# The order of the first DMA loads on SyncE and ScalarE: two quarters of unit 0 ahead of the positions and frequencies

## Chip, cores, metric

The kernel runs on one core of a Trainium2 chip. The metric is the time on the device in microseconds (us), as a median of several runs. A profile shows one execution, from its first to its last instruction. This span is 1.7 to 2.1 us shorter than the time of the same execution, and times inside a profile count from its start.

## The reference, cut to what matters

```python
# x (8, 8, 1024, 64) float32, freqs (32,), positions 0..1023, scale 0.5
angles = np.outer(positions * scale, freqs)
cos, sin = np.cos(angles), np.sin(angles)
x_first, x_second = x[..., :32], x[..., 32:]
out_first  = x_first * cos - x_second * sin
out_second = x_first * sin + x_second * cos
```

16.8 MB are read and 16.8 MB are written. The table of sines and cosines comes out of two tiny inputs, 8 KB of positions and 128 bytes of frequencies, and everything else waits for it.

## The kernel before

x is cut into four units of 128 rows by 8192 elements. GpSimd's DMAs convert to float16 while they load. Only the second half of unit 0 is loaded as float32, in two quarters of 1 MB by SyncE and ScalarE, into X0f; ScalarE converts it later. `pin` fixes the order of the instructions on their engine.

```python
    X0f = xout.tile([P, N], FP32, tag="O")
    Q = NH // 2                                    # 2048 elements, 8 KB of each row
    pin(nc.sync.dma_start(out=X0f[:, :Q], in_=xv[0][:, NH : NH + Q]))        # SyncE's quarter

    pos_i64 = consts.tile([P, K8], positions.dtype)
    pin(nc.scalar.dma_start(out=pos_i64, in_=positions.rearrange("(p k) -> p k", k=K8)))
    freq_row = consts.tile([1, half], FP32)
    pin(nc.scalar.dma_start(out=freq_row, in_=freqs[None, :]))
    pin(nc.scalar.dma_start(out=X0f[:, Q:NH], in_=xv[0][:, NH + Q :]))       # ScalarE's quarter
    ...
    pin(nc.gpsimd.dma_start(out=Xf[0][:, :NH], in_=xv[0][:, :NH]))           # first half of unit 0
    ...  # constants by GpSimd
    for u in range(1, NU):                         # units 1 to 3, the last one in two pieces
        ...
        pin(nc.gpsimd.dma_start(out=Xf[u][:, : N - c], in_=xv[u][:, : N - c]))
    ...
    # cfreq = coef x freq_row (TensorE); posf = float(positions); y = posf * cfreq (VectorE)
    # tab = sines and cosines (ScalarE); T = tab spread over the rows (TensorE, copies by ScalarE, VectorE)
    pin(nc.scalar.copy(out=Xf[0][:, NH:], in_=X0f[:, :NH]))
    for u in range(NU):
        for s in range(2):                         # half units
            ...                                    # four VectorE operations, then OUT <- X on ScalarE
            # stores: units 0 and 3 by SyncE for each half, units 1 and 2 by GpSimd as a whole
```

The positions are 128 records of 64 bytes, one for each row, eight on each of the 16 DMA engines. A quarter is 128 records of 8 KB, also eight for each engine.

Of the kernel before, what the change touches and what calls it, by code (L numbers as in the profile page):

```python
# [21 lines left out]
def kernel(  # L22
# [8 lines left out]
    nc = tc.nc  # L31
    pin = tc.keep_in_program_order
# [11 lines left out]
    NH = KH * D  # L44
    K8 = S // P
# [7 lines left out]
    xv = x.rearrange("b h s d -> (b h s d)").rearrange("(u p n) -> u p n", p=P, n=N)  # L53
# [11 lines left out]
    X0f = xout.tile([P, N], FP32, tag="O")  # L65
    Q = NH // 2
    pin(nc.sync.dma_start(out=X0f[:, :Q], in_=xv[0][:, NH : NH + Q]))

    pos_i64 = consts.tile([P, K8], positions.dtype)
    pin(nc.scalar.dma_start(out=pos_i64, in_=positions.rearrange("(p k) -> p k", k=K8)))  # L70
    freq_row = consts.tile([1, half], FP32)
    pin(nc.scalar.dma_start(out=freq_row, in_=freqs[None, :]))
    pin(nc.scalar.dma_start(out=X0f[:, Q:NH], in_=xv[0][:, NH + Q :]))

    X = [xin.tile([P, K, 2, half], FP16, name=f"X{u}") for u in range(NU)]
    Xf = [t.rearrange("p k h j -> p (k h j)") for t in X]
# [12 lines left out]
        out=one, in_=one, compare_op=ALU.not_equal, fill=1.0, base=0,  # L89
        pattern=[[-1, G], [-G, HP]], channel_multiplier=1,  # L90
    ))
    for u in range(1, NU):
# [12 lines left out]
        out=posf, in_=pos_i64.bitcast(I32).rearrange("p (k t) -> p k t", t=2)[:, :, 0]  # L105
# [3 lines left out]
        out=y,  # L109
# [8 lines left out]
        out=r, in0=m, scalar=_MAGIC, in1=y, op0=ALU.subtract, op1=ALU.subtract  # L118
# [5 lines left out]
        out=ra.bitcast(I32), in0=r.bitcast(I32), scalar1=0x7FFFFFFF, scalar2=None, op0=ALU.bitwise_and  # L124
# [5 lines left out]
    for g in range(0, G, 2):  # L130
        ps = spread.tile([P, 2, 2, W], FP32, tag="g")
        for i in range(2):
            nc.tensor.matmul(  # L133
                out=ps[:, i].rearrange("p t w -> p (t w)"),
# [12 lines left out]
    for u in range(NU):  # L147
        OUT = xout.tile([P, N], FP32, tag="O")
        for s in range(2):
# [9 lines left out]
                out=Xs[:, :, 0, :], in0=Xs[:, :, 0, :], in1=pr[:, :, 1, :], op=ALU.subtract  # L159
            ))  # L160
            pin(nc.vector.tensor_tensor(  # L161
                out=Xs[:, :, 1, :], in0=pr[:, :, 0, :], in1=Xs[:, :, 1, :], op=ALU.add
# [39 lines left out]
```

## Time and profile before

| | before |
|---|---|
| time, median of 6 runs | 84.39 us (84.19 to 84.59) |
| span of the profile | 82.4 us |
| busy: VectorE, ScalarE, TensorE | 60.3, 40.1, 6.0 us |
| shares of the three DMA queues together | 97.3% of the span |

VectorE works back to back in the middle of the span, and the DMA engines are full almost from end to end. The lines that carry this stand in the prediction. The queues: q0 is GpSimd's, q1 SyncE's, q10 ScalarE's (the prediction calls the last two the HWDGE rings); a ring is what one queue has on one DMA engine. The columns are packets, MB written, and share of the 16 engines' time.

```profile
q1 hardware_dynamic: 720, 9.44, 27.5%
q10 hardware_dynamic: 290, 1.06, 3.3%
```

### The profile page before, as it was taken

The page shows a single profiled execution, that of the slowest core. Times are in us where ns is not written, and L with a number is a line of the kernel's source. Part 1 is how long each engine was busy: PE and PEld are TensorE (multiplying, and loading weights), DVE is VectorE, ACT ScalarE, POOL GpSimd, SP SyncE. Part 2 cuts the span into 40 slices and gives each one's busy share as a digit, 9 for nine tenths or more (in the row PEclk, how much of TensorE's full clock was granted, in tenths as well). Part 3 has the DMA queues.
Part 4 walks back from the last instruction along what each step waited for, and adds up shares of the span by engine and source line. Part 5 has one row for each costly group of instructions (what it writes and reads, how often), then busy time and mean ns, then how long its engine had stood idle before and what let it go on. Part 6 is the DMA issues. An engine that isn't in the chain of part 4 may idle for free.

```text
span 82.4 us, 183 instructions
## 1 busy us (share of the span) xinstructions
PE 6.0 (7%) x18; PEld 2.4 (3%) x18; DVE 60.3 (73%) x40; ACT 40.1 (49%) x18; POOL 5.1 (6%) x15
## 2 busy tenths in 40 slices
PE   0011797100000000000000000000000000000000
PEld 0011232000000000000000000000000000000000
DVE  0306277999999999999999999999999998000000
ACT  0602259999950690294088049309705911950000
POOL 4950000000000000000000200000110000000000
PEclk9999999995555555555555555555555555555555
DMA  2899997996996999899899899997995998989992
GB/s 44 345 312 286 282 350 167 255 255 143 239 255 127 255 255 334 302 308 280 239 322 266 239 398 330 545 430 334 509 509 255 509 509 350 414 382 469 422 414 95
DMA packets 2018, 26.22 MB, mean 318 GB/s; under 512 B 354, under 2 KB 354, under 8 KB 482
## 3 DMA queue, kind: packets, MB, share of 16 engines
q0 software_dynamic: 1008, 15.73, 66.5%
q1 hardware_dynamic: 720, 9.44, 27.5%
q10 hardware_dynamic: 290, 1.06, 3.3%
HBM read 16.79 MB, written 16.78 MB: 407 GB/s over the span
## 4 chain that ended last, share of the span: by engine, by line
DVE 54%; ACT 15%; issue 7%; DMA 6%; PE 5%; DVEq 1%; ACTq 0%
DVE X L157 20%; DVE pr L156 20%; DVE X L161 9%; DMA freq_row<-in_freqs_dram 6%; ACT T L143 5%; DVE X L158 5%; ACT OUT L164 4%; ACT X L144 4%; PE ps L133 4%; DVEq L197 1%; PE cfreq L101 1%; ACT tab L126 1%; DVE r L117 1%; DVE y L108 1%; ACTq L70 0%
## 5 line engine op out<-in xcount | busy, mean ns | idle before, releaser
L164 ACT CAST OUT<-X 128x4096 f32<-128x4096 f16 x8 | 28.8, 3606 | 24.2 <-DVE X L161 24.2
L156 DVE TENSOR_TENSOR pr<-X,T 128x4096 f16<-128x4096 f16 x8 | 18.3, 2292 | 0.8 <-ACT T L143 0.5
L157 DVE TENSOR_TENSOR X<-X,T 128x4096 f16<-128x4096 f16 x8 | 18.3, 2292 | 0.3
L158 DVE TENSOR_TENSOR X<-X,pr 128x2048 f16<-128x2048 f16 x8 | 9.8, 1224 | 0.3
L161 DVE TENSOR_TENSOR X<-pr,X 128x2048 f16<-128x2048 f16 x8 | 9.7, 1217 | 0.0
L143 ACT CAST T<-ps 128x1024 f16<-128x1024 f32 x6 | 5.7, 1030 | 2.4 <-PE ps L133 2.4
L133 PE MATMUL ps<-tab,sel 128*128 128x512 f16 x16 | 5.4, 489 | 2.8 <-ACT tab L126 2.2
L168 POOL DMA_DIRECT2D out_dram<-OUT x2 | 1.1, 537 | 53.7 <-ACT OUT L164 53.7
L141 DVE CAST T<-ps 128x1024 f16<-128x1024 f32 x2 | 2.4, 1224 | 2.2 <-PE ps L133 2.2
L144 ACT CAST X<-X0f 128x4096 f16<-128x4096 f32 x1 | 3.6, 3650 | 0.0
L99 DVE COPY sel<-one 128x2048 f16<-128x2048 f16 x1 | 0.7, 693 | 2.8 <-POOL one L88 2.8
L121 ACT ACTIVATE tab<-r 128x256 f16<-128x256 f32 x1 | 0.4, 416 | 4.4 <-DVE r L117 4.4
L121 ACT ACT_TABLE_LOAD x1 | 1.3, 1283 | 2.1 <-issue 2.1
L133 PEld LDWEIGHTS <-sel 128*128 128x128 f16 x16 | 1.9, 120 | 5.9 <-issue 5.3
L94 POOL DMA_DIRECT2D X<-in_x_dram x3 | 2.0, 659 | 0.0
L104 DVE CAST posf<-pos_i 128x8 f32<-128x8 int32 x1 | 0.2, 171 | 2.1 <-DMA pos_i<-in_positions_dram 2.1
L101 PE MATMUL cfreq<-freq_row,coef 1*128 1x32 f32 x2 | 0.6, 392 | 5.9 <-DMA freq_row<-in_freqs_dram 5.9
L108 DVE TENSOR_TENSOR y<-posf,cfreq 128x256 f32<-128x256 f32 x1 | 0.4, 423 | 0.7 <-PE cfreq L101 0.7
L84 POOL DMA_DIRECT2D X<-in_x_dram x1 | 0.7, 667 | 0.8 <-POOLq L183 0.8
L101 PEld LDWEIGHTS cfreq<-freq_row,coef 1*128 1x128 f32 x2 | 0.5, 306 | 5.9 <-issue 5.9
L96 POOL DMA_DIRECT2D X<-in_x_dram x1 | 0.6, 558 | 0.0
L126 ACT ACTIVATE tab<-ra,quarter 128x256 f16<-128x256 f32 x1 | 0.5, 507 | 0.0
(11 smaller groups left out, 2.3 us busy)
## 6 DMA issues: line engine op xcount, KB each, us to landing
out_dram<-OUT SPq DMA_DIRECT2D x4, 2048.0 KB, 14.2
out_dram<-OUT POOLq DMA_DIRECT2D x2, 4096.0 KB, 14.8
X<-in_x_dram POOLq DMA_DIRECT2D x2, 2048.0 KB, 25.7
X<-in_x_dram POOLq DMA_DIRECT2D x1, 1792.0 KB, 44.6
X0f<-in_x_dram SPq DMA_DIRECT2D x1, 1024.0 KB, 4.7
X<-in_x_dram POOLq DMA_DIRECT2D x1, 1024.0 KB, 11.5
X0f<-in_x_dram ACTq DMA_DIRECT2D x1, 1024.0 KB, 13.4
X<-in_x_dram POOLq DMA_DIRECT2D x1, 256.0 KB, 47.7
```

Of the source, the lines that this page charges most:

```text
L94: pin(nc.gpsimd.dma_start(out=Xf[u][:, : N - c], in_=xv[u][:, : N - c]))
L101: nc.tensor.matmul(out=cfreq, lhsT=coef, rhs=freq_row, start=True, stop=True)
L121: pin(nc.scalar.activation(out=tab[:, 0], in_=r, func=AF.Sin, bias=0.0, scale=-_TWO_PI_DN))
L133: nc.tensor.matmul(out=ps[:, i].rearrange("p t w -> p (t w)"), lhsT=sel[:, g + i].rearrange("s h q -> s (h q)"), rhs=tab.rearrange("s t k ...
L141: pin(nc.vector.tensor_copy(out=dst, in_=ps))
L143: pin(nc.scalar.copy(out=dst, in_=ps))
L144: pin(nc.scalar.copy(out=Xf[0][:, NH:], in_=X0f[:, :NH]))
L156: pin(nc.vector.tensor_tensor(out=pr, in0=Xs, in1=sin_b, op=ALU.mult))
L157: pin(nc.vector.tensor_tensor(out=Xs, in0=Xs, in1=cos_b, op=ALU.mult))
L158: pin(nc.vector.tensor_tensor(out=Xs[:, :, 0, :], in0=Xs[:, :, 0, :], in1=pr[:, :, 1, :], op=ALU.subtract))
L161: pin(nc.vector.tensor_tensor(out=Xs[:, :, 1, :], in0=pr[:, :, 0, :], in1=Xs[:, :, 1, :], op=ALU.add))
L164: pin(nc.scalar.copy(out=OUT[:, ns], in_=Xf[u][:, ns]))
```

## The change

The intent: both issuing engines begin at once with a large transfer, and ScalarE's quarter no longer stands behind two small loads.

```diff
     pin(nc.sync.dma_start(out=X0f[:, :Q], in_=xv[0][:, NH : NH + Q]))
+    pin(nc.scalar.dma_start(out=X0f[:, Q:NH], in_=xv[0][:, NH + Q :]))
 
     pos_i64 = consts.tile([P, K8], positions.dtype)
-    pin(nc.scalar.dma_start(out=pos_i64, in_=positions.rearrange("(p k) -> p k", k=K8)))
+    pin(nc.sync.dma_start(out=pos_i64, in_=positions.rearrange("(p k) -> p k", k=K8)))
     freq_row = consts.tile([1, half], FP32)
     pin(nc.scalar.dma_start(out=freq_row, in_=freqs[None, :]))
-    pin(nc.scalar.dma_start(out=X0f[:, Q:NH], in_=xv[0][:, NH + Q :]))
```

## The prediction

> **What bounds the kernel now.** I read the chain of waits first, because the change touches only the first six microseconds and the question is whether those lie on it.
>
> ```profile
> 1.16 4.61 DMA freq_row<-in_freqs_dram
> 5.90 0.61 PE cfreq L101 x2
> 6.54 0.43 DVE y L108
> ...
> 8.74 3.38 PE ps L133 x8
> 12.14 3.08 ACT T L143 x4
> ...
> 16.82 3.50 ACT X L144
> 20.35 2.31 DVE pr L156
> ...
> 69.67 3.60 ACT OUT L164
> ```
>
> Columns: start, length (us), work. The end is tied rigidly to the landing of the 128-byte frequencies: cfreq, y, the sine table, its spreading by TensorE, the copies into T, the conversion of X0f (L144), and from 20.35 on VectorE back to back. So what delays y delays everything behind it. The timeline names the other input of y, and what the first rotation waits for:
>
> ```profile
> 5.63 0.17 DVE L104 CAST posf<-pos_i 128x8 f32<-128x8 int32 x1 [2.14 <-DMA pos_i<-in_positions_dram]
> 6.54 0.42 DVE L108 TENSOR_TENSOR y<-posf,cfreq 128x256 f32<-128x256 f32 x1 [0.74 <-PE cfreq L101]
> 13.19 2.29 DVE L156 TENSOR_TENSOR pr<-X,T 128x4096 f16<-128x4096 f16 x1 [0.47 <-ACT T L143]
> 16.67 3.65 ACT L144 CAST X<-X0f 128x4096 f16<-128x4096 f32 x1
> ```
>
> Positions came 0.3 us before the frequencies; either can become the gate. L144 has no wait on its line: ScalarE is busy with T until then, and X0f is there already. Next the transfers, by issue and by stretch (last two columns of the second view: DMA share, GB/s written):
>
> ```profile
> X<-in_x_dram POOLq DMA_DIRECT2D x1, 1024.0 KB, 11.5
> X0f<-in_x_dram SPq DMA_DIRECT2D x1, 1024.0 KB, 4.7
> X0f<-in_x_dram ACTq DMA_DIRECT2D x1, 1024.0 KB, 13.4
> pos_i<-in_positions_dram ACTq DMA_DIRECT2D x1, 8.0 KB, 4.9
> ```
>
> ```profile
> 1.75:5.80 4.05, 0.00 (x0) 0.00 (x0) 0.86 (x2) 1.28 (x1) 3.37 (x9) 1.00 1.02 332
> 5.80:13.20 7.40, 4.83 (x14) 2.12 (x15) 3.90 (x7) 2.97 (x5) 0.00 (x0) 1.00 1.03 278
> 20.40:69.65 49.25, 0.00 (x0) 0.00 (x0) 48.56 (x28) 25.07 (x7) 1.07 (x2) 0.50 1.01 335
> 73.30:82.40 9.10, 0.00 (x0) 0.00 (x0) 0.00 (x0) 0.00 (x0) 0.00 (x0) 0.50 0.81 346
> ```
>
> The 16 DMA engines are full from 1.75 us nearly to the end, so the kernel stands close to two limits: compute and its last store, and a DMA backlog. The two quarters, equal in size, take 4.7 and 13.4 us: a transfer costs what its place in its ring and its neighbours cost, not what its bytes cost.
>
> **What the Trainium skill says.** "DMA: Bandwidth & Descriptors", section "Queues, rings and completion order": each of the 16 engines has one ring per queue, consumes a ring in order, and goes round-robin over the rings that have work, one packet per turn. The trace's packet records agree. Until about 4.7 us each engine alternates an 8 KB packet of SyncE's quarter with a 64-byte packet of the positions, one for one, although one takes 0.31 us and the other 0.01. Later it alternates ScalarE's quarter with GpSimd's load. Near 13.3 us an 8 KB packet is followed by one 1.21 us GpSimd packet before the 4-byte completion of the same ring gets its turn. So **a turn costs what the neighbour's packet costs, however small one's own is.** The same page, section "Why a DMA increments its semaphore by 16 and not by 1": only the full count means that all has landed. Hence the slowest engine counts for the positions (128 rows, eight on each engine); the frequencies are one record on one engine. Same page, "Latency and other measured facts": first byte about 1 us for GpSimd's DMA. The trace doesn't agree here: issued at 1.25, its first packet starts at 4.71.
>
> **The change, part by part.**
>
> Removed: positions (0.39 us of issuing) and frequencies (0.55) no longer stand ahead of ScalarE's quarter, which is issued at 0.74 instead of 1.74. Nothing on the chain waits for that quarter, so its gain is zero.
>
> Added: positions behind SyncE's quarter, frequencies behind ScalarE's. No compute instruction changes; VectorE, TensorE and GpSimd have the same order as before, and ScalarE and SyncE differ only in those issues.
>
> Cost, as seen by one middling engine, with packet times from the records (8 KB plain 0.31 us; 8 KB written by the casting load, which reads twice that, 0.61; 16 KB written by it 1.21):
> - First packets from about 2.0. Before, eight plain packets were through by 4.8; now these eight are four of each quarter. I assume that GpSimd's load enters at 4.75, as before.
> - Four rounds of all three rings, 0.61 + 0.31 + 0.31 = 1.23 us each: both quarters end at 9.7.
> - The quarters' completion packets need a turn behind the fifth GpSimd packet: 10.3.
> - Positions one to three follow GpSimd's packets six to eight, at 10.9, 11.5, 12.1. The fourth comes with that load's own completion. Then GpSimd's ring goes on with unit 1, whose packets take 1.21: positions five to eight at 13.3, 14.5, 15.8, 17.0, and their completion at 18.2. Slowest engine and landing add about 0.5, so 18.7.
> - If GpSimd enters one round later, one 1.21 turn drops out: about 17.5. I take **18.3 for the positions, against 5.6**.
> - Frequencies need only two turns behind their quarter on one engine: about 12.
>
> Then posf (0.17) and gaps: y starts at about 18.5 instead of 6.54, **a shift of 12.0 us**. Everything on the chain behind it keeps its lengths. GpSimd's loads go on during this, so X never becomes the wait.
>
> At the end: the last store is issued at 73.3 + 12.0 = 85.3. Alone it would need about 1.0 to start, 8 x 0.62 = 5.0 per engine, and 0.4 to land: 91.7, where before it landed at 81.5. But backlog remains: unit 2's store is issued at 59.5 + 12.0 = 71.5, starts perhaps 2 us later (estimate, between the skill's 1 and the 3.5 seen), and from there 16 + 8 + 8 packets of 0.62 = 19.8 us end at 93.3, landing at 93.7. With the 0.9 us that follow the last landing in the trace before, the span is 94.6. The timed runs lie 1.95 above the span (84.35 against 82.4): 96.5. Without that backlog: 94.6. I put **96.2**.
>
> **Rivals.**
> - *The small transfers slip in early.* If GpSimd's load can't enter while the HWDGE rings have work, both quarters run at the 0.31 us pace and end near 7.3, with positions and frequencies at about 7.5. For it: on each engine GpSimd's first packet directly follows the end of SyncE's quarter, as if it had waited for that; and it started late. Against it: from 5.4 to 12.4 it alternates one for one with ScalarE's quarter, which never ran empty in that time. Also, a newcomer waits behind packets already scheduled: the first store, issued at 23.86, has its first packet only at 28.5, behind two or three loads. The shift would be 1 to 1.5 us; the last store now ends some 1.8 us later than it would alone, so most of that would hide: 84.3 to 85.7, within 2%.
> - *Earlier X0f gains time.* ScalarE's quarter lands at some 10 instead of 15.2 us. But L144 starts when ScalarE is free at 16.67, and its order on ScalarE is fixed behind the copies into T. Gain nil; this is the only way to faster and I see nothing for it.
> - *The delay is hidden by DMA.* The engines were the second limit, and work moved from the start isn't lost. But stores depend on compute: all loads together are about 39 us of engine time, done by about 42, while the second store comes at 43 and the third only at 57, so the engines run dry for several us before unit 1's store. This can hide no more than the 1.8 us above.
>
> **Range and chances.** Given turn-taking with three rings (I hold it for 85% likely), entry of GpSimd's load a round earlier or later moves the shift to 11 to 13, and the backlog moves the end by 2: 93.5 to 98.5. The first rival is most of the rest. Range 92.5 to 98.8; slower by over 2% 0.86, within 2% 0.12, faster 0.02.
>
> **What would show it.** The wait of posf on the positions grows from 2.14 to about 15 us, and the chain begins with positions in place of frequencies. Issue to landing: positions some 17 us, SyncE's quarter near 9 instead of 4.7, ScalarE's about 9 instead of 13.4. Between 5 and 18 us PE, VectorE and ScalarE show almost nothing; behind it the same groups with the same mean durations, and slices with low DMA share in the second half. What would make it wrong: positions landing by 8 us (the first rival), or frequencies later than positions.

## The result

The changed kernel takes 95.13 us (94.7 to 95.24, 6 runs) against 84.39 for the one before. The ratio is 1.126, with a 95% interval of 1.123 to 1.129. Here and below a ratio is the mean time of one kernel's runs over that of the other's of the same rounds, so it is not quite the ratio of the medians. Executions over 1.5% slower than the fastest of the same kernel are left out of the means.

The chain of waits of the changed kernel (start, length, work) begins with the positions:

```profile
1.18 16.77 DMA pos_i<-in_positions_dram
...
17.97 0.18 DVE posf L104
...
18.25 0.43 DVE y L108
...
20.44 3.59 PE ps L133 x8
...
32.26 2.30 DVE pr L156
```

Before, y began at 6.54; now it begins at 18.25, 11.71 us later. From there on the links are the same. The timeline of the changed kernel shows that the frequencies were not the gate, and how far the first rotation has moved:

```profile
10.89 0.60 PE L101 MATMUL cfreq<-freq_row,coef 1*128 1x32 f32 x2 [10.89 <-DMA freq_row<-in_freqs_dram]
17.97 0.17 DVE L104 CAST posf<-pos_i 128x8 f32<-128x8 int32 x1 [14.48 <-DMA pos_i<-in_positions_dram]
...
25.09 2.29 DVE L156 TENSOR_TENSOR pr<-X,T 128x4096 f16<-128x4096 f16 x1 [0.67 <-ACT T L143]
```

The frequencies were there 7 us before the positions, whose wait on VectorE grew from 2.14 to 14.48 us. The first rotation starts 11.90 us later than before (25.09 against 13.19). The 0.2 us more than at y fell to TensorE's spreading of the table, whose matmuls took 596 ns in the mean instead of 489.

The transfers of the changed kernel, with the time from issue to landing in the last column:

```profile
X0f<-in_x_dram ACTq DMA_DIRECT2D x1, 1024.0 KB, 10.0
X0f<-in_x_dram SPq DMA_DIRECT2D x1, 1024.0 KB, 9.9
...
pos_i<-in_positions_dram SPq DMA_DIRECT2D x1, 8.0 KB, 16.8
```

The two quarters, 4.7 and 13.4 us before, now take the same time, as two rings in turn would. ScalarE's quarter is on the chip 4.4 us earlier (0.74 + 10.0 against 1.74 + 13.4), and nothing uses it: its conversion starts at 28.57. The queues of the changed kernel:

```profile
q1 hardware_dynamic: 864, 9.45, 24.6%
q10 hardware_dynamic: 146, 1.05, 2.8%
```

Exactly 144 packets have moved from q10 to q1, with 0.01 MB: 128 records of positions and 16 completions. Each record is a packet of its own. The packet records of the trace show the turns. As medians over the 16 engines, SyncE's quarter ends at 9.0 and ScalarE's at 9.3; a position follows at 10.5, 11.1, 11.7, each behind a 0.62 us packet of GpSimd's first load, two at 12.2 and 12.4, where that load ends, and then one at 13.5, 14.8 and 16.0, each behind a packet of unit 1 of some 1.2 us. Their completion, a 4-byte packet that reports the landing, goes at 17.2; on the slowest engine it goes at 17.6.

The end grew less than the start: the span by 11.0 us, the first rotation by 11.9. The kernel before had a backlog of transfers at its end that hid 0.9. Behind it the DMA engines now run dry, as this stretch of the changed kernel and then of the one before shows (the last two columns are the DMA share and GB/s written; each share is the mean over the 18 us, in which nearly idle stretches and full ones alternate):

```profile
57.00:75.00 18.00, 0.00 (x0) 0.00 (x0) 17.73 (x12) 7.63 (x4) 1.07 (x2) 0.50 0.71 304
```

```profile
57.00:75.00 18.00, 0.00 (x0) 0.00 (x0) 12.47 (x8) 9.40 (x3) 0.53 (x1) 0.50 0.97 419
```

### The profile page after: what moved, and what is told of

Read it like the earlier page. It is cut to its first block, busy times and chain, and to the rows that moved or that the text cites. A ratio compares the mean times of both kernels' runs of the same rounds, so it can differ in the third digit from the quotient of the medians.

```text
span 93.4 us, 183 instructions
## 1 busy us (share of the span) xinstructions
PE 7.1 (8%) x18; PEld 2.8 (3%) x18; DVE 60.3 (65%) x40; ACT 40.1 (43%) x18; POOL 5.1 (6%) x15
## 4 chain that ended last, share of the span: by engine, by line
DVE 48%; DMA 18%; ACT 13%; issue 6%; PE 4%; DVEq 1%; SPq 0%; ACTq 0%
DMA pos_i<-in_positions_dram 18%; DVE X L157 17%; DVE pr L156 17%; DVE X L161 8%; ACT T L143 4%; DVE X L158 4%; ACT OUT L164 4%; PE ps L133 4%; ACT X L144 4%; DVEq L197 1%; ACT tab L126 1%; DVE r L117 0%; DVE y L108 0%; SPq L67 0%; ACT tab L121 0%
## 5 line engine op out<-in xcount | busy, mean ns | idle before, releaser
L156 DVE TENSOR_TENSOR pr<-X,T 128x4096 f16<-128x4096 f16 x8 | 18.3, 2292 | 1.0 <-ACT T L143 0.7
L157 DVE TENSOR_TENSOR X<-X,T 128x4096 f16<-128x4096 f16 x8 | 18.3, 2292 | 0.3
L133 PE MATMUL ps<-tab,sel 128*128 128x512 f16 x16 | 6.5, 596 | 8.9 <-ACT tab L126 8.9
L101 PE MATMUL cfreq<-freq_row,coef 1*128 1x32 f32 x2 | 0.6, 390 | 10.9 <-DMA freq_row<-in_freqs_dram 10.9
L101 PEld LDWEIGHTS cfreq<-freq_row,coef 1*128 1x128 f32 x2 | 0.5, 308 | 10.9 <-issue 10.9
## 6 DMA issues: line engine op xcount, KB each, us to landing
out_dram<-OUT POOLq DMA_DIRECT2D x2, 4096.0 KB, 11.7
```

The costliest lines, as they stand in the source:

```text
L133: nc.tensor.matmul(out=ps[:, i].rearrange("p t w -> p (t w)"), lhsT=sel[:, g + i].rearrange("s h q -> s (h q)"), rhs=tab.rearrange("s t k ...
L156: pin(nc.vector.tensor_tensor(out=pr, in0=Xs, in1=sin_b, op=ALU.mult))
L157: pin(nc.vector.tensor_tensor(out=Xs, in0=Xs, in1=cos_b, op=ALU.mult))
```

## The experiments

Theory: the positions pay one neighbour's packet for each of their own packets, however small they are; they were through early before because SyncE's plain 8 KB packets (0.31 us) were the only neighbour, and they pay GpSimd's packets (0.61, then 1.21 us) now. Rivals: the wait is one for bytes, or for a share of the bandwidth; or the mere place behind a quarter is what costs, for the frequencies as well. All eight kernels compute the right result, and each was timed over three rounds.

### The neighbour's packets made smaller

```diff
     for u in range(1, NU):
         c = C2 if u == NU - 1 else 0
+        if u == 1:
+            for b in range(0, N, N // 4):
+                pin(nc.gpsimd.dma_start(out=Xf[u][:, b : b + N // 4], in_=xv[u][:, b : b + N // 4]))
+            continue
```

> The changed kernel, with GpSimd's load of unit 1 in four pieces by columns: the same bytes, ring and order, but packets of 4 KB written (0.31 us) in place of 16 KB (1.21 us). Theory (the positions pay a neighbour's packet for each turn; four of their turns fell behind unit 1's packets): positions land 4 x 0.9 = 3.6 us earlier, near 14.3 instead of 17.95, time about 91.5 us (90.5 to 92.5). Rival (the positions wait for bytes ahead of them or for their share of the bandwidth, which are unchanged): 95 us.

Measured: 91.44 us, ratio 1.084 to the kernel before. The positions landed 12.9 us after their issue instead of 16.8:

```profile
14.13 0.17 DVE L108 CAST posf<-pos_i 128x8 f32<-128x8 int32 x1 [10.64 <-DMA pos_i<-in_positions_dram]
```

That is 3.84 us earlier than in the changed kernel, where the theory said 3.6, and the time fell by 3.7. The same bytes in the same order on the same ring: the bandwidth rival has no place for this.

### The positions cut into twice as many packets

```diff
-    pin(nc.sync.dma_start(out=pos_i64, in_=positions.rearrange("(p k) -> p k", k=K8)))
+    pv = positions.rearrange("(p k) -> p k", k=K8)
+    pin(nc.sync.dma_start(out=pos_i64[:, : K8 // 2], in_=pv[:, : K8 // 2]))
+    pin(nc.sync.dma_start(out=pos_i64[:, K8 // 2 :], in_=pv[:, K8 // 2 :]))
```

> The changed kernel, with the positions (still 8 KB in all) loaded by two DMAs of four columns each, both behind SyncE's quarter: 16 small packets and two completions on each engine instead of 8 and one. Theory (turns): nine more turns behind GpSimd's 1.21 us packets, 10.9 us: positions land near 28.9 instead of 17.95, time 105 to 107 us. Rival (the wait is set by the quarter ahead and by bytes): within 1 us of 95.

Measured: 105.55 us, ratio 1.249.

```profile
27.61 0.17 DVE L106 CAST posf<-pos_i 128x8 f32<-128x8 int32 x1 [24.12 <-DMA pos_i<-in_positions_dram]
```

The same 8 KB came 9.64 us later and the time grew by 10.4; of the other 0.7, 0.4 lie behind the last conversion (8.7 us from there to the end instead of 8.3), where nothing was changed and what made it longer was not looked for, and 0.3 outside the span. So it is the number of packets that counts, not the bytes. The nine turns expected would have been 10.9 us; the landing shows eight (9.64 / 1.21 = 8.0). The packet records show where the ninth is: near 21.9 one turn fell on the 4-byte completion of unit 1's load instead of a 1.21 us packet, which I had overlooked.

### The neighbour held back

GpSimd reads one column of posf before it issues its loads, so it can't enter before the positions are in.

```diff
-    pin(nc.gpsimd.dma_start(out=Xf[0][:, :NH], in_=xv[0][:, :NH]))     # and the loop over units 1 to 3
 ...
+    gate = consts.tile([P, 1], FP32)
+    pin(nc.gpsimd.tensor_copy(out=gate, in_=posf[:, :1]))
+    pin(nc.gpsimd.dma_start(out=Xf[0][:, :NH], in_=xv[0][:, :NH]))     # then the loop
```

> The changed kernel, with all of GpSimd's loads held back until posf is made (GpSimd reads one column of it first). Theory (the positions wait for GpSimd's packets, not for the quarters): both quarters end near 7.0, positions land at about 7.5 instead of 17.95, y at about 7.8. The price is an idle stretch of the DMA engines of some 2 us from 7.1 to 9.2, since GpSimd's first packet comes about 1.1 us after its issue: time 85.3 to 87.5 us. Rival (a small transfer of 64-byte records is slow behind any quarter): positions well beyond 10 us, time above 90.

Measured: 87.79 us, ratio 1.041. The wait of the positions and the stretch of the DMA engines after it:

```profile
8.40 0.17 DVE L98 CAST posf<-pos_i 128x8 f32<-128x8 int32 x1 [6.09 <-DMA pos_i<-in_positions_dram]
```

```profile
7.30:10.10 2.80, 0.60 (x2) 0.60 (x3) 1.41 (x5) 0.07 (x1) 1.47 (x4) 1.00 0.04 3
```

Behind the same quarter, without GpSimd's packets, the positions land at 8.4 instead of 17.95. That settles who makes them wait. The time missed its forecast by 0.3 us: I had put the idle stretch at 2 us, and it was 2.8 with a slow start behind it (first packets of 0.76 to 1.62 us in place of 0.62). The loss against the kernel before is 3.4 us. It is no longer the positions' doing: the first rotation now waits for GpSimd's own load, held back, and starts 3.5 us later than before (16.67 against 13.19):

```profile
16.67 2.29 DVE L159 TENSOR_TENSOR pr<-X,T 128x4096 f16<-128x4096 f16 x1 [1.70 <-DMA X<-in_x_dram]
```

### Only one of the two small loads moved

With the positions ahead again:

```diff
+    pin(nc.sync.dma_start(out=pos_i64, in_=...))        # ahead of SyncE's quarter
     pin(nc.sync.dma_start(out=X0f[:, :Q], ...))
     pin(nc.scalar.dma_start(out=X0f[:, Q:NH], ...))
-    pin(nc.sync.dma_start(out=pos_i64, in_=...))
     pin(nc.scalar.dma_start(out=freq_row, in_=freqs[None, :]))
```

> The changed kernel, but the positions stand ahead of SyncE's quarter again; the frequencies stay behind ScalarE's quarter. Theory (the positions were the gate of the changed kernel; the frequencies need two turns only): positions land by about 6 us, the frequencies near 10.8 as in the changed kernel, and they become the gate: y at about 11.5 instead of 18.25 (before: 6.54), time 88.4 us (87.5 to 89.5). Rival (both small transfers cost about the same; the harm is that something small is behind a quarter at all): close to 95 us.

With the frequencies ahead again:

```diff
+    pin(nc.scalar.dma_start(out=freq_row, in_=freqs[None, :]))   # ahead of ScalarE's quarter
     pin(nc.sync.dma_start(out=X0f[:, :Q], ...))
     pin(nc.scalar.dma_start(out=X0f[:, Q:NH], ...))
     pin(nc.sync.dma_start(out=pos_i64, in_=...))
-    pin(nc.scalar.dma_start(out=freq_row, in_=freqs[None, :]))
```

> The changed kernel, but the frequencies stand ahead of ScalarE's quarter again; the positions stay behind SyncE's quarter. Theory: the frequencies had 7 us to spare in the changed kernel, so nothing changes: positions land near 17.5 to 18, y at about 18, time 94 to 95.5 us. Rival (the frequencies cost something of their own): visibly below 95, by 2 us or more.

Both expectations failed. Measured: 84.25 us with the positions ahead (ratio 0.999) and 84.24 with the frequencies ahead (0.999), the time of the kernel before. The transfers of the first of them (positions ahead), then of the second:

```profile
X0f<-in_x_dram ACTq DMA_DIRECT2D x1, 1024.0 KB, 4.7
X0f<-in_x_dram SPq DMA_DIRECT2D x1, 1024.0 KB, 11.6
...
pos_i<-in_positions_dram SPq DMA_DIRECT2D x1, 8.0 KB, 2.8
```

```profile
X0f<-in_x_dram SPq DMA_DIRECT2D x1, 1024.0 KB, 4.6
...
X0f<-in_x_dram ACTq DMA_DIRECT2D x1, 1024.0 KB, 11.4
...
pos_i<-in_positions_dram SPq DMA_DIRECT2D x1, 8.0 KB, 4.3
```

In each, one quarter took 4.6 or 4.7 us, as if it were alone. In the second the positions stand behind SyncE's quarter just as in the changed kernel, and landed 4.3 us after their issue instead of 16.8. The issues of the quarters suggest why (start and length; first with the positions ahead, then with the frequencies ahead):

```profile
0.74 0.40 ACTq L70 DMA_DIRECT2D X0f<-in_x_dram  x1
...
1.16 0.43 SPq L69 DMA_DIRECT2D X0f<-in_x_dram  x1
```

```profile
0.74 0.37 SPq L69 DMA_DIRECT2D X0f<-in_x_dram  x1
...
1.30 0.36 ACTq L70 DMA_DIRECT2D X0f<-in_x_dram  x1
```

The later ring's first 8 KB packet came at 4.71 and 4.83, when the earlier ring's quarter was through. So the quarter that led by 0.42 or 0.56 us had the engines to itself, and what stood behind it went out before GpSimd's load came in at 5.2. With the frequencies ahead, the positions did not even pay a turn each: all 128 records went between 4.76 and 5.05, and in that time ScalarE's quarter, issued at 1.30, began at most one 0.31 us packet on each engine. So the turn for each record is what the changed kernel and its first two variants show, and no rule for every busy neighbour. My expectations had simply carried over the turn-taking of the changed kernel, where both quarters are issued at 0.74.

### The same two with the quarters issued together again

If that is so, one more small load that nobody reads, ahead of the other quarter, must bring the loss back.

```diff
     # to the kernel with the frequencies ahead
+    freq_idle = consts.tile([1, half], FP32)
+    pin(nc.sync.dma_start(out=freq_idle, in_=freqs[None, :]))           # ahead of SyncE's quarter
     # to the kernel with the positions ahead
+    pos_idle = consts.tile([P, K8], positions.dtype)
+    pin(nc.scalar.dma_start(out=pos_idle, in_=positions.rearrange("(p k) -> p k", k=K8)))   # ahead of ScalarE's
```

> As e2_freq_first (frequencies ahead of ScalarE's quarter, positions behind SyncE's), with one more 128-byte load, into a tile that nobody reads, ahead of SyncE's quarter, so that both quarters are issued in the same moment again (near 1.3 us). New theory (a ring that starts half a microsecond earlier gets the engines to itself until its quarter is through at about 4.8; only quarters issued together take turns, end after GpSimd's load has entered, and leave the positions to its packets): positions land near 17.5 to 18.5, time 94 to 96 us. Rival (positions behind a quarter are harmless as long as the frequencies are ahead of the other one): 84.2 us, as e2_freq_first.

Measured: 94.70 us, ratio 1.122. A 128-byte load that nobody reads costs 10.5 us:

```profile
17.25 0.17 DVE L106 CAST posf<-pos_i 128x8 f32<-128x8 int32 x1 [13.76 <-DMA pos_i<-in_positions_dram]
```

> As e1_pos_first (positions ahead of SyncE's quarter, frequencies behind ScalarE's), with a second load of the positions, into a tile that nobody reads, ahead of ScalarE's quarter, so that both rings carry the same again and both quarters are issued near 1.2 us. New theory: the quarters take turns, the frequencies come two turns behind the end of ScalarE's at 11 to 12.5 us and are the gate: y at 11.6 to 13, time 88.5 to 90.5 us. Rival (frequencies behind a quarter are harmless as long as the positions are ahead of the other one): 84.3 us, as e1_pos_first.

Measured: 89.93 us, ratio 1.068:

```profile
12.00 0.60 PE L103 MATMUL cfreq<-freq_row,coef 1*128 1x32 f32 x2 [12.00 <-DMA freq_row<-in_freqs_dram]
```

Both hold in time, and the frequencies also in y (12.64, said 11.6 to 13); the positions of the first landed at 17.23, 0.3 us before their range. The quarters of the first were level only in part, for SyncE's was still issued 0.14 us ahead:

```profile
1.14 0.36 SPq L71 DMA_DIRECT2D X0f<-in_x_dram  x1
...
1.28 0.37 ACTq L72 DMA_DIRECT2D X0f<-in_x_dram  x1
```

In the second kernel the frequencies alone are behind, and their price with turn-taking quarters is seen by itself: y at 12.64 instead of 6.54, and 5.5 us of time. They are one packet on one engine; the positions, eight on each engine, cost 10.3 (94.70 less 84.42).

### Both small loads ahead of both quarters

```diff
+    pin(nc.sync.dma_start(out=pos_i64, in_=...))
+    pin(nc.scalar.dma_start(out=freq_row, in_=freqs[None, :]))
     pin(nc.sync.dma_start(out=X0f[:, :Q], ...))
     pin(nc.scalar.dma_start(out=X0f[:, Q:NH], ...))
-    # the two small loads behind them
```

> Positions ahead of SyncE's quarter, frequencies ahead of ScalarE's, both quarters behind them. Both small transfers land by 3 to 5.5 us, so y comes up to 3 us earlier than before (6.54). Theory (DMA engines full from 1.75 us on are the second limit of the kernel before, and the first rotation then waits for GpSimd's half of unit 0 at about 12.6): no gain, 83.8 to 84.5 us. Rival (the landing of the small transfers alone sets the end): 81.5 to 82.5 us.

Measured: 84.73 us, ratio 1.004 (1.002 to 1.007). No gain, as the theory said, but 0.2 us above its range.

```profile
3.69 0.42 DVE L107 TENSOR_TENSOR y<-posf,cfreq 128x256 f32<-128x256 f32 x1
13.77 2.29 DVE L155 TENSOR_TENSOR pr<-X,T 128x4096 f16<-128x4096 f16 x1 [3.82 <-DMA X<-in_x_dram]
```

y comes 2.85 us earlier than before, and the first rotation later (13.77 against 13.19): it waits for GpSimd's half of unit 0. In this kernel both quarters are ahead of that half in part, since it entered at 5.86 and later, against 4.71 in the kernel before. None of the eight is clearly faster than the kernel before.

## Why the prediction was right

It was right in time (96.2 against 95.13, range 92.5 to 98.8) and in its mechanism, for this kernel. By its own steps:

- **Gate.** It said that either small input could become the gate, and that it would be the positions. The chain begins with them, and the kernels in which they come early are not slow by them.
- **Turns.** It said that a position pays a neighbour's packet. Smaller neighbours, more packets and no neighbour each moved the landing as that says: 3.84 us earlier (3.6 said), 9.64 later (10.9 said), to 8.4 (7.5 said).
- **Landing of the positions.** 18.3 said, 17.95 measured. The round that it left open came out late: GpSimd's load entered at 5.39 to 6.1 on the different engines, not at 4.75. For the same reason the frequencies were earlier than said (10.9 against about 12).
- **Shift.** 12.0 said; 11.71 at y, 11.90 at the first rotation.
- **End.** Unit 2's store was to start 2 us after its issue, as an estimate between the skill's 1 and the 3.5 seen. It started at 72.49, 1.1 after its issue at 71.39. These 0.9 us are most of the 1.2 by which the span (93.4) lies under the 94.6 said. From there to the last landing at 92.55 it took 20.1 us (19.8 and 0.4 said). The six timed runs lie 1.73 to 1.84 above their spans, not 1.95: that figure had set the time of one execution against the span of another (the profiled one took 84.16, 1.8 above its 82.4). The backlog hid 0.9 us; at most 1.8 was said.
- **Rivals.** The small transfers did not slip in early: GpSimd's load entered while both other rings had work. An earlier X0f gained nothing.

One thing the prediction took for granted without saying that it mattered: that the two quarters take turns because they are issued in the same moment. Two later expectations failed on just this. Here the edit happened to issue both at 0.74; that the turns depend on it the prediction did not know, and to that extent it was lucky. Its view that the place behind a quarter costs so much was borne out only for quarters issued within 0.14 us of each other, with GpSimd's load coming in behind them.

What stays open is why a lead of 0.42 us decides. The runs show that the lead works by degrees. With SyncE's quarter issued 0, 0.10, 0.14 and 0.56 us ahead of ScalarE's (the changed kernel, both small loads ahead, the idle frequencies, the frequencies ahead), ScalarE's first packet on any engine started at 2.14, 3.62, 3.90 and 4.83. By then 14, 30, 55 and all 128 packets of SyncE's quarter had started, or about 1, 2, 3.4 and 8 for each engine. That the engines take in packets ahead, and share out only what is not yet taken in, would fit this. It would also fit the positions that went out in one run, GpSimd's late entry, and the first store of the kernel before, issued at 23.86 with its first packet at 28.5. It was argued only, not tested. Nor was a lead made in any other way than by a small load in front of a quarter. That the rings carried unlike small loads is not enough by itself: with both small loads ahead they did, the lead was 0.10, and the quarters took 9.8 and 10.6 us.

## What to carry to other kernels

Put a small load that a chain waits for ahead of the large ones on its ring. Behind them it can pay, for each of its records, a whole packet of the ring that is busy beside it, as the positions did beside GpSimd's load, so count its records and the neighbour's packet time, not its bytes. Where a small load is behind a large one all the same, check when the rings are issued against each other: here half a microsecond of lead, or one useless 128-byte load, decided over 10 us. In this kernel, whose DMA engines are already full almost from end to end, an earlier start of the table gained nothing.

## What the Trainium skill lacked or had wrong

- "DMA: Bandwidth & Descriptors", section "Queues, rings and completion order": the round-robin by packets holds once the rings share an engine, but the page lacks its price for small transfers. The 8 KB of positions landed 16.8 us after issue beside GpSimd's packets, 12.9 with unit 1's packets a quarter as large, and 7.2 without them.
- The same section calls 9 to 17 descriptors in a packet typical. Here each 64-byte record counted as a packet in the trace (moving 128 of them with 16 completions moved exactly 144 packets from one queue to the other) and took a turn of its own beside GpSimd's load.
- The same section doesn't say when a ring that comes later gets its first turn. Behind a quarter issued 0.42 or 0.56 us earlier, the first packet of the second quarter came 3.5 us after its issue (1.16 to 4.71, 1.30 to 4.83), when the first was through, and the 128 positions behind the first quarter went before it or beside its first packet (4.76 to 5.05); quarters issued together alternated from their second packet on.
- The same page, section "Latency and other measured facts", first byte of GpSimd's DMA about 1 us: found on idle engines (1.1 us for unit 2's store, 1.4 in the kernel with the neighbour held back), but 3.5 to 4.8 us at the start of the kernels in which the other rings were full (issued at 1.25, first packet at 4.71 in the kernel before and at 6.01 with the idle positions). The page gives no figure for that.
- The same page, section "Issuing engines are not separate DMA queues", says that issuing from several engines saves only the sequencer's time. For bandwidth no run here speaks against it; but which ring a small load is on, and what is issued beside it, moved this kernel's time between 84.2 us (frequencies ahead) and 95.1 (the changed kernel).
